# Moving sums, copies and transposes of a transformer block between waits: first sum, delta rule, FFN input, last quarters by token

## The chip, the cores and the metric

The kernel runs on one core of a Trainium2 chip. A core has TensorE (PE, matmuls and transposes), VectorE (DVE), ScalarE (ACT), GpSimd (POOL) and SyncE (SP, which here issues nearly all loads), each with its own instruction queue, and 16 DMA engines that they share. The metric is the device time of one execution in microseconds (us), the median of several.

## The reference, cut to what matters

One layer of a bidirectional encoder, 256 tokens of 2048 channels, all in float32. Two branches run on the same projected input and are merged; a SwiGLU feed-forward part (FFN) follows.

```python
c_act = silu(c)                                   # one row of 2048
mod = c_act @ ada_w + ada_b                       # 6 x 2048: shift, scale, gate of mixer and of FFN
h = rms_norm(x, norm_mix_w) * (1 + scale_m) + shift_m
proj = h @ w_in                                   # q, k, v, gates of both branches
h_a = bidirectional(mlstm_chunkwise, ...)         # branch A: 4 heads, q/k 256, v 512
y_a = (sigmoid(a_o) * rms_norm(h_a)) @ w_branch_a
o_b = bidirectional(gated_delta_chunkwise, ...)   # branch B: 16 heads of 128, gated delta rule
y_b = (rms_norm(o_b) * silu(b_z)) @ w_branch_b
x = x + gate_m * ((g_a * y_a + g_b * y_b) @ w_out)
hf = rms_norm(x, norm_ffn_w) * (1 + scale_f) + shift_f
gt, up = split(hf @ w_gate_up)                    # 2 x 5632
x = x + gate_f * ((silu(gt) * up) @ w_down)
return rms_norm(x, norm_final_w)
```

The delta rule of a chunk needs the inverse of a triangular 64x64 matrix per head, chunk and direction; that is the work called inversion below.

## The kernel before, in words

**Precision.** Every float32 weight matmul is done as three matmuls of a faster 32-bit type: an operand is split into a rounded high part and the rest, and high x high, high x low and low x high are summed. Weights come by 1 MB loads into one ring of three buffers (`raw`); for each half (8 blocks of 128x128, or 2 of 128x512) ScalarE makes the high part (`wh`) and VectorE the low part (`wl`), each in a ring of three. `fjob` (L131, names `b`, `a`) gives outputs with channels on the partitions, two halves to a load; `tjob` (L153, names `z`, `v`, `ma`, `mb`, `o`, `gt`, `up`, `d`) gives outputs with tokens on the partitions: a half is 12 matmuls of 128x512, 6 for each of two token tiles, which end at the same chunk.

**Modulation.** `mod` is not made by TensorE. A row of c is spread over all partitions (`crow`); then for each block of 128 outputs the transposed weights are loaded (1 MB) and VectorE forms one product sum (128x2048, L110 for the parts 2 to 5, L443 and L445 for shift and scale of the mixer). The parts 2 to 5 are a background list: `pump()` is called once for each finished load of weights, and takes one sum of that list at each `every[0]`-th call. The loads of the sums use the `raw` ring and SP's queue as the weights do.

**Stages.** (1) The start, L400 to L455: x is loaded, squared, transposed by TensorE into pxx, copied to x; for each of the 16 channel blocks the two sums, x scaled and shifted, split into hh and hl, and the first 16 projections (`first`). (2) The rest of the projections of branch B in `fill` steps and pieces of a `stream`, between the steps of the delta rule. There are four groups `g` of four heads; each has `gdn_invert` (vector products of small matrices that were reordered through DRAM, inst_d to uu), `gdn_blocks` (copies that lay blocks of 32 rows and columns into R, X and UL) and two pairs `p` of heads in `gdn_phase2`: a chain of small matmuls, copies and products in ten steps, of which the last transposes the normed output (px), scales it (obt, ScalarE) and stores it. `after` and `last` give how many pieces come between two of the steps. (3) mLSTM (branch A), whose head inputs are loaded back from DRAM by SP, between `fill` steps of ma and mb. (4) y_b, y_a, then the output projection o0 to o3 with the residual, each of them one `tjob` for 512 channels. (5) The FFN: x1 is normed (xn), transposed (pxn), scaled and shifted (hf), split into hfh and hfl, two blocks of 128 channels at a time; then gt0, up0, gt1, up1 and so on for 11 groups of 512 channels; then d0 to d3 with the second residual, the final norm and the output.

**What sets the order.** Instructions wrapped in `order(...)` stay as written on their engine's queue; all others are placed by a planner that takes what is ready by its own costs. An engine's queue is strictly in order on the chip: what stands behind a waiting instruction waits with it. `fill(n)` issues n halves of the next projections, `invert(g)` calls it ahead of the inversion.

The line numbers of the profile are those of this kernel. Lines that the prediction's steps touch: L414 to L431 (start), L612 to L616 (UL), L709 to L717 (px and obt), L791 to L796 (invert), L806 (every), L963 to L968 (mLSTM's start), L1021 to L1044 (residual, root, o), L1057 to L1076 (FFN input), L1103 to L1110 (tail).

Of the kernel before, what the change touches and what calls it, by code (L numbers as in the profile page):

```python
# [15 lines left out]
P = 128  # L16
T = 256
# [35 lines left out]
def hybrid_block(ctx: ExitStack, tc: tile.TileContext, xr, nfr, crow, pk_d, cst_d, ada2, ada4, win0, winb, wint, wba, wbb, wo, wgu, wd, out, dbg=None):  # L53
# [44 lines left out]
    for g in range(4):  # L98
        pc_ = acc_ps.tile([P, 512], F32, tag="acc", name=f"crow{g}")
        PE.matmul(pc_, ones[0:1], c1[:, g * 512 : (g + 1) * 512], start=True, stop=True)  # L100
        S.activation(row_c[:, g * 512 : (g + 1) * 512], pc_, AF.Silu)
# [51 lines left out]
    def tjob(name, chunks, xh, xl, done, early=0):  # L153
# [16 lines left out]
        made = [halves(*q) for q in todo[:early]]  # L170
        if early:
            yield True
        ps = [acc_ps.tile([P, 512], F32, tag="acc", name=f"acc_{name}_{t}") for t in range(2)]
        last = 4 * len(chunks) - 1
        for u, k0 in todo:
            wh, wl = made.pop(0) if made else halves(u, k0)
            for k in range(2):
                kk = 4 * u + k0 + k
                for t in range(2):
                    c = slice(t * P, (t + 1) * P)  # L180
                    PE.matmul(ps[t], xh[:, kk, c], wh[:, k], start=kk == 0, stop=False)  # L181
                    PE.matmul(ps[t], xl[:, kk, c], wh[:, k], start=False, stop=False)  # L182
                    PE.matmul(ps[t], xh[:, kk, c], wl[:, k], start=False, stop=kk == last)  # L183
            if k0:
                pump()
                if u == len(chunks) - 1:
                    done(ps)
            yield True

# [215 lines left out]
    with ExitStack() as s0:  # L405
# [9 lines left out]
        junk = w0.tile([P, D + 2], F32, tag="ra", bufs=5, name="junk")  # L415
        for t in range(2):
            order(S.activation(junk[:, :D], xt[t][:, :D], AF.Square, accum_out=ss[:, t : t + 1]))
        order(S.activation(ss, ss, AF.Sqrt, bias=epsc, scale=1.0 / D))
        for b2 in range(KB // 2):
            px = gps(f"pxx{b2}")  # L420
            for e in range(2):
                for t in range(2):
                    PE.transpose(px[:, e * T + t * P : e * T + (t + 1) * P], xt[t][:, (2 * b2 + e) * P : (2 * b2 + e + 1) * P], ident)
            V.tensor_copy(x[:, 2 * b2 : 2 * b2 + 2], px.rearrange("p (e t) -> p e t", e=2))
        V.reciprocal(ss, ss)
        dg = w0.tile([P, T], F32, name="dgx")
        for t in range(2):
            V.tensor_scalar(dg[:, t * P : (t + 1) * P], ident, ss[:, t : t + 1], None, ALU.mult)
        prow = acc_ps.tile([P, 512], F32, tag="acc", name="prow")
        PE.matmul(prow[:, :T], ones, dg, start=True, stop=True)  # L430
# [4 lines left out]
        for b in range(KB):  # L435
            ra = [w0.tile([P, D + 2], F32, tag="ra", bufs=5, name=f"ra{b}_{i}") for i in range(2)]
            raw = st.tile([P, N0, P], F32, tag="raw", bufs=3, name=f"raw0_{b}")
            for i in range(2):
                order(nc.sync.dma_start(ra[i], ada2[b, :, i]))
            order(nc.sync.dma_start(raw, win0[b]))  # L440
            m2 = w0.tile([P, 2], F32, tag="m2", bufs=3, name=f"m2_{b}")
            f = pk[:, PK_NMIX + b : PK_NMIX + b + 1]
            order(V.scalar_tensor_tensor(ra[0], ra[0], f, row_c, ALU.mult, ALU.mult, accum_out=m2[:, 0:1]))  # L443
            order(V.scalar_tensor_tensor(x[:, b], x[:, b], m2[:, 0:1], rows, ALU.mult, ALU.mult))
            order(V.scalar_tensor_tensor(ra[1], ra[1], 1.0, row_c, ALU.mult, ALU.mult, accum_out=m2[:, 1:2]))  # L445
# [145 lines left out]
    def gdn_blocks(g):  # L591
# [20 lines left out]
        for i, a in enumerate((F_, B_)):  # L612
            for b in range(4):
                r = slice(32 * b, 32 * b + 32)
                order(S.activation(UL[r, i, :, r], a[r], AF.Copy))
            yield  # L616

    def gdn_phase2(g, p):
# [91 lines left out]
        for e, on in enumerate(ons):  # L710
            h, hl_ = 4 * g + 2 * p + e, 2 * p + e
            for t in range(2):
                PE.transpose(px[:, (2 * e + t) * P : (2 * e + t + 1) * P], on[:, t], ident)
            obt = bk.tile([P, T], F32, tag="obt", bufs=2, name=f"obt{h}")
# [76 lines left out]
    def invert(g):  # L791
        gen = gdn_invert(g)
        next(gen)
        fill(4)
# [4 lines left out]
    for g in range(4):  # L799
# [6 lines left out]
        every[0] = (0, 2, 2, 2)[g]  # L806
        for p in range(2):
            pieces = stream(4 * g + 2 * p + 4)
# [157 lines left out]
    fill(2)  # L966
    next(cores)
    fill(6)  # L968
# [52 lines left out]
    def residual(t, g, ps, gate, ss, rp):  # L1021
        c = slice(g * 512, (g + 1) * 512)
        tm = rp.tile([P, 512], F32, tag="tm", bufs=2, name=f"tm{ss.name}_{t}_{g}")
        V.tensor_tensor(tm, ps, gate[:, c], ALU.mult)
        V.tensor_tensor(x1[:, t, c], x1[:, t, c], tm, ALU.add)
        S.activation(tm, x1[:, t, c], AF.Square, accum_out=ss[:, t, g : g + 1])

    def token_rstd(ss, name):
        rs = xp.tile([P, 2], F32, name=name)
        V.tensor_reduce(rs, ss, mybir.AxisListType.X, ALU.add)  # L1030
        S.activation(rs, rs, AF.Sqrt, bias=epsc, scale=1.0 / D)
        V.reciprocal(rs, rs)
        return rs

    ss1 = xp.tile([P, 2, 4], F32, name="ss1")
    for g in range(4):
        every[0] = 1 if g in (1, 2) else 2
        run(tjob(f"o{g}", [wo[g, u] for u in range(4)], mgh, mgl, lambda ps: [residual(t, g, ps[t], gm, ss1, wp) for t in range(2)]))
# [4 lines left out]
    every[0] = 4  # L1043
    rs = token_rstd(ss1, "rs1")  # L1044
# [9 lines left out]
    hfl = hp.tile([P, KB, T], F32R, name="hfl")  # L1054
    ffh = fp.tile([P, FB, T], F32R, name="ffh")
    ffl = fp.tile([P, FB, T], F32R, name="ffl")
    for q in range(4):  # L1057
        xn = hp.tile([P, 2, 512], F32, tag="sg", bufs=2, name=f"xn{q}")
        for t in range(2):
            V.tensor_scalar(xn[:, t], x1[:, t, q * 512 : (q + 1) * 512], rs[:, t : t + 1], None, ALU.mult)  # L1060
        for e2 in range(2):
            px = gps(f"pxn{q}_{e2}")
            hf = hp.tile([P, 2, T], F32, tag="hf", bufs=1, name=f"hf{q}_{e2}")
            for e in range(2):
                f = 2 * e2 + e
                for t in range(2):
                    PE.transpose(px[:, e * T + t * P : e * T + (t + 1) * P], xn[:, t, f * P : (f + 1) * P], ident)
                b = 4 * q + f
                V.tensor_scalar(
                    hf[:, e],  # L1070
                    px[:, e * T : (e + 1) * T],
                    affn[:, b : b + 1],
                    mod[:, 3 * KB + b : 3 * KB + b + 1],
                    ALU.mult,
                    ALU.add,
                )  # L1076
            b = 4 * q + 2 * e2
            split(hfh[:, b : b + 2], hfl[:, b : b + 2], hf)

    for j in range(FB // 4):  # L1080
        sg = hp.tile([P, 2, 512], F32, tag="sg", bufs=2, name=f"sg{j}")
        run(tjob(f"gt{j}", [wgu[j, 0, u] for u in range(4)], hfh, hfl,
                 lambda ps: [S.activation(sg[:, t], ps[t], AF.Silu) for t in range(2)]))
# [19 lines left out]
    for g in range(4):  # L1103
        run(tjob(f"d{g}", [wd[g, u] for u in range(KD)], ffh, ffl, lambda ps: [residual(t, g, ps[t], gf, ss2, dp) for t in range(2)]))
    rs = token_rstd(ss2, "rs2")
    for g in range(4):
        c = slice(g * 512, (g + 1) * 512)
        for t in range(2):
            V.scalar_tensor_tensor(x1[:, t, c], x1[:, t, c], rs[:, t : t + 1], nf[:, c], ALU.mult, ALU.mult)
        nc.sync.dma_start(out[:, :, c], x1[:, :, c])  # L1110
# [101 lines left out]
```

## Time and profile before

| | |
|---|---|
| median of 3 runs | 2104.58 us (2102.53 to 2105.44) |
| profiled execution | 2102.55 us, span 2100.8 us |
| mean granted clock of TensorE | 0.986 |
| busy: TensorE, VectorE, ScalarE, GpSimd | 2034.4, 1404.8, 1042.3, 95.8 us |
| loaded from HBM, mean rate | 467 MB, 230 GB/s |

The profile is one execution. Each of its groups names the line, the engine, the operation, the tile written and the tiles read, then how many, busy time and the mean of one in ns, then the engine's idle time just before them and what ended it. "PE px L713 <- ACT obt L715" means that TensorE's instruction of line 713 waited until ScalarE's of line 715 was done. A window row gives for a stretch its length, the busy time of each engine, the clock that was granted to TensorE as a share of full speed, the share of the DMA engines that was busy, and GB/s. Matmuls overlap, so one of them shows a longer time than it adds.

### The profile page before, as it was taken

The page shows a single profiled execution, that of the slowest core. Times are in us where ns is not written, and L with a number is a line of the kernel's source. Part 1 is how long each engine was busy: PE and PEld are TensorE (multiplying, and loading weights), DVE is VectorE, ACT ScalarE, POOL GpSimd, SP SyncE. Part 2 cuts the span into 40 slices and gives each one's busy share as a digit, 9 for nine tenths or more (in the row PEclk, how much of TensorE's full clock was granted, in tenths as well). Part 3 has the DMA queues.
Part 4 walks back from the last instruction along what each step waited for, and adds up shares of the span by engine and source line. Part 5 has one row for each costly group of instructions (what it writes and reads, how often), then busy time and mean ns, then how long its engine had stood idle before and what let it go on. Part 6 is the DMA issues. An engine that isn't in the chain of part 4 may idle for free.

```text
span 2100.8 us, 26981 instructions
## 1 busy us (share of the span) xinstructions
PE 2034.4 (97%) x10374; PEld 1702.8 (81%) x10374; DVE 1404.8 (67%) x2065; ACT 1042.3 (50%) x1546; POOL 95.8 (5%) x189
## 2 busy tenths in 40 slices
PE   8999999999999999999999999899999999999997
PEld 6877789978988888889777877688888888878885
DVE  6787686787877687865677678765556554454544
ACT  2146548756774677565444443344444444444442
POOL 0002210110111011100000000000000000000000
PEclk9999999999999999999999999999999999999999
DMA  9986665566766565767886688566666765555553
GB/s 384 420 315 205 170 210 162 171 189 243 225 195 213 178 213 211 236 247 255 321 298 235 260 288 326 192 220 223 257 223 222 257 206 195 184 198 199 190 190 120
DMA packets 81971, 485.65 MB, mean 231 GB/s; under 512 B 10521, under 2 KB 20001, under 8 KB 27441
## 3 DMA queue, kind: packets, MB, share of 16 engines
q1 hardware_dynamic: 68672, 459.34, 60.9%
q0 software_dynamic: 5856, 9.49, 2.9%
q10 hardware_dynamic: 7314, 15.10, 1.9%
q8 instruction: 81, 1.33, 0.3%
q14 instruction: 48, 0.39, 0.1%
HBM read 467.07 MB, written 16.82 MB: 230 GB/s over the span
## 4 chain that ended last, share of the span: by engine, by line
PE 80%; DVE 7%; DMA 6%; ACT 4%; issue 2%; POOL 0%; SPq 0%; DVEq 0%; ACTq 0%; POOLq 0%
PE acc_gt L181 4%; PE acc_gt L182 4%; PE acc_up L181 4%; PE acc_up L182 4%; PE acc_d L181 4%; PE acc_up L183 4%; PE acc_d L182 4%; PE acc_d L183 4%; PE acc_gt L183 4%; PE first L452 3%; PE acc_b L147 2%; PE acc_b L145 2%; PE acc_b L146 2%; PE acc_o L183 2%; PE acc_o L181 2%; PE acc_o L182 2%
## 5 line engine op out<-in xcount | busy, mean ns | idle before, releaser
L166 DVE TENSOR_TENSOR wl_d<-raw_d,wh_d 128x1024 fp32r<-128x1024 f32 x88 | 107.9, 1226 | 123.2 <-ACT wh_d L165 123.2
L166 DVE TENSOR_TENSOR wl_up<-raw_up,wh_up 128x1024 fp32r<-128x1024 f32 x88 | 107.9, 1226 | 111.7 <-ACT wh_up L165 111.7
L145 PE MATMUL acc_b<-hh,wh_b 128*128 128x256 f32 x576 | 165.2, 287 | 4.7 <-ACT wh_b L141 4.7
L110 DVE SCALAR_TENSOR_TENSOR ada<-ada,crow 128x2048 f32<-128x2048 f32 x64 | 146.4, 2288 | 28.4 <-DMA ada<-ada 28.2
L166 DVE TENSOR_TENSOR wl_gt<-raw_gt,wh_gt 128x1024 fp32r<-128x1024 f32 x88 | 107.2, 1225 | 86.6 <-ACT wh_gt L165 86.6
L147 PE MATMUL acc_b<-hh,wl_b 128*128 128x256 f32 x576 | 162.3, 282 | 1.1 <-DVE wl_b L142 1.1
L165 ACT ACTIVATE wh_d<-raw_d 128x1024 fp32r<-128x1024 f32 x88 | 93.3, 1061 | 138.9 <-PE acc_d L182 134.0
L146 PE MATMUL acc_b<-hl,wh_b 128*128 128x256 f32 x576 | 161.2, 280 | 0.0
L165 ACT ACTIVATE wh_gt<-raw_gt 128x1024 fp32r<-128x1024 f32 x88 | 93.3, 1060 | 133.9 <-PE acc_gt L182 73.4
L165 ACT ACTIVATE wh_up<-raw_up 128x1024 fp32r<-128x1024 f32 x88 | 93.3, 1060 | 117.8 <-PE acc_up L182 82.5
L181 PE MATMUL acc_gt<-wh_gt,hfh 128*128 128x512 f32 x352 | 138.8, 397 | 2.7 <-ACT hfh L205 2.4
L182 PE MATMUL acc_gt<-wh_gt,hfl 128*128 128x512 f32 x352 | 139.4, 396 | 0.0
L183 PE MATMUL acc_gt<-wl_gt,hfh 128*128 128x512 f32 x352 | 138.6, 394 | 0.0
L181 PE MATMUL acc_d<-wh_d,ffh 128*128 128x512 f32 x352 | 137.5, 391 | 0.0
L182 PE MATMUL acc_d<-wh_d,ffl 128*128 128x512 f32 x352 | 137.4, 390 | 0.0
L183 PE MATMUL acc_d<-wl_d,ffh 128*128 128x512 f32 x352 | 137.0, 389 | 0.0
L183 PE MATMUL acc_up<-wl_up,hfh 128*128 128x512 f32 x352 | 136.9, 389 | 0.0
L181 PE MATMUL acc_up<-wh_up,hfh 128*128 128x512 f32 x352 | 136.9, 389 | 0.0
L182 PE MATMUL acc_up<-wh_up,hfl 128*128 128x512 f32 x352 | 136.9, 389 | 0.0
L452 PE MATMUL first<-x,raw 128*128 128x256 f32 x512 | 115.1, 387 | 6.7 <-ACT x L446 6.7
L452 PEld LDWEIGHTS first<-x,raw 128*128 128x128 f32 x512 | 98.7, 194 | 23.0 <-ACT x L446 9.3
L145 PEld LDWEIGHTS acc_b<-hh,wh_b 128*128 128x128 f32 x576 | 110.2, 191 | 5.1 <-ACT wh_b L141 5.1
(345 smaller groups left out, 5256.8 us busy)
## 6 DMA issues: line engine op xcount, KB each, us to landing
ada<-ada SPq DMA_DIRECT2D x64, 1024.0 KB, 5.0
raw_gt<-wgu SPq DMA_DIRECT2D x44, 1024.0 KB, 5.0
raw_up<-wgu SPq DMA_DIRECT2D x44, 1024.0 KB, 4.9
raw_d<-wd SPq DMA_DIRECT2D x44, 1024.0 KB, 4.9
raw_b<-winb SPq DMA_DIRECT2D x36, 1024.0 KB, 5.1
ra<-ada SPq DMA_DIRECT2D x32, 1025.0 KB, 14.6
raw<-win SPq DMA_DIRECT2D x16, 1024.0 KB, 12.8
raw_z<-wint SPq DMA_DIRECT2D x16, 1024.0 KB, 4.9
```

The source lines that it names most:

```text
L110: V.scalar_tensor_tensor(raw, raw, 1.0, row_c[:, :D], ALU.mult, ALU.mult, accum_out=mod[:, c0 + b : c0 + b + 1])
L145: PE.matmul(o, wh[:, k], hh[:, kk], start=kk == 0, stop=False)
L146: PE.matmul(o, wh[:, k], hl[:, kk], start=False, stop=False)
L147: PE.matmul(o, wl[:, k], hh[:, kk], start=False, stop=kk == KB - 1)
L165: order(S.activation(wh, raws[u][:, k0 : k0 + 2], AF.Copy), early)
L166: order(V.tensor_tensor(wl, raws[u][:, k0 : k0 + 2], wh.bitcast(F32), ALU.subtract), early)
L181: PE.matmul(ps[t], xh[:, kk, c], wh[:, k], start=kk == 0, stop=False)
L182: PE.matmul(ps[t], xl[:, kk, c], wh[:, k], start=False, stop=False)
L183: PE.matmul(ps[t], xh[:, kk, c], wl[:, k], start=False, stop=kk == last)
L452: PE.matmul(first[o], raw[:, o], x[:, b], start=b == 0 and o % 2 == 0, stop=b == KB - 1 and o % 2 == 1)
```

## The change

- **Start.** c's row is made in four parts by `c_row`; the square of token tile 0 (ScalarE) stands between the first and the others, that of tile 1 goes to VectorE. `junk`, the squares' unused output, moves from a slot of the `ra` ring into hl, which is written later. The first loads and the sum of scale for block 0 stand ahead of the transposes; the copies of x move from VectorE to ScalarE; the transposes stand behind the scaling of the identity.
- **Delta rule.** Six halves instead of four ahead of the first inversion; the copies of UL's second half (`i == 1`) on VectorE; both heads' transposes ahead of both obt copies; background sums at no piece in the first pair and at each in the second, where they were at every second piece of both (group 0 has none, before and after).
- **mLSTM.** Four halves ahead of the cores' first step, four behind it, instead of two and six.
- **Output projection.** Three sums in each of o0 to o3, at fixed steps. In o3 and d3 the last quarter of the weights (two halves) is done for token tile 0 and then for tile 1 (`by_token`); the residual, the root and, in d3, the final scaling and the output stores of each tile follow its own matmuls. `root()` issues a square root of a constant ahead of o3 and d3. gt0's first two halves are made during o3.
- **FFN input by blocks** of 128 channels with a written order in which each step of gt0 (one half) is issued between the blocks; one in two of the later hf goes to ScalarE. The sums of part 5 begin after gt0.
- **Tail.** nf is multiplied in under the next job for d0 to d2; the output goes in eight parts of 256 KB instead of four of 512 KB.

```diff
+    def c_row(g):
+        order(PE.matmul(pc_, ones[0:1], c1[:, g * 512 : (g + 1) * 512], start=True, stop=True))
+        order(S.activation(row_c[:, g * 512 : (g + 1) * 512], pc_, AF.Silu))
...
-    def tjob(name, chunks, xh, xl, done, early=0):
+    def tjob(name, chunks, xh, xl, done, early=0, by_token=False, steps=1):
...
-        for u, k0 in todo:
+        if by_token:
+            todo = todo[:-2]
+        for n, (u, k0) in enumerate(todo):
             wh, wl = made.pop(0) if made else halves(u, k0)
+            if early and steps > 1 and n + early < len(todo):
+                made.append(halves(*todo[n + early]))
...
+        if by_token:
+            w = [halves(len(chunks) - 1, k0) for k0 in (0, 2)]
+            for t in range(2):
+                for k in range(4):
+                    kk = last - 3 + k
+                    wh, wl = (a[:, k % 2] for a in w[k // 2])
+                    PE.matmul(ps[t], xh[:, kk, c], wh, start=False, stop=False)
...
+                done(t, ps[t])
...
-        junk = w0.tile([P, D + 2], F32, tag="ra", bufs=5, name="junk")
+        junk = hl.rearrange("p b t -> p (b t)")
+        c_row(0)
+        order(S.activation(junk[:, :D], xt[0][:, :D], AF.Square, accum_out=ss[:, 0:1]))
+        for g in (1, 2, 3):
+            c_row(g)
+        order(V.scalar_tensor_tensor(junk[:, D : 2 * D], xt[1][:, :D], 1.0, xt[1][:, :D], ALU.mult, ALU.mult, accum_out=ss[:, 1:2]))
+        order(S.activation(ss, ss, AF.Sqrt, bias=epsc, scale=1.0 / D))
...
+        ra, raw = loads(0)
+        m2 = scale(0, ra)
+        order(V.reciprocal(ss, ss))
...
-            V.tensor_copy(x[:, 2 * b2 : 2 * b2 + 2], px.rearrange("p (e t) -> p e t", e=2))
+            order(S.activation(x[:, 2 * b2 : 2 * b2 + 2], px.rearrange("p (e t) -> p e t", e=2), AF.Copy))
...
-                order(S.activation(UL[r, i, :, r], a[r], AF.Copy))
+                if i:
+                    order(V.tensor_copy(UL[r, i, :, r], a[r]))
+                else:
+                    order(S.activation(UL[r, i, :, r], a[r], AF.Copy))
...
                 PE.transpose(px[:, (2 * e + t) * P : (2 * e + t + 1) * P], on[:, t], ident)
+        for e in range(2):
+            h, hl_ = 4 * g + 2 * p + e, 2 * p + e
             obt = bk.tile([P, T], F32, tag="obt", bufs=2, name=f"obt{h}")
...
-        fill(4)
+        fill(4 if g else 6)
...
-        every[0] = (0, 2, 2, 2)[g]
         for p in range(2):
+            every[0] = p if g else 0
...
-    fill(2)
+    fill(4)
     next(cores)
-    fill(6)
+    fill(4)
...
+        if g == 3:
+            root()
+        for i, _ in enumerate(tjob(f"o{g}", [wo[g, u] for u in range(4)], mgh, mgl, done_o, by_token=g == 3)):
+            if i in ((2, 4, 6) if g < 3 else (1, 2, 4)):
+                sums()
+            if g == 3 and i == 6:
+                next(gt0)
...
+    def moved(b):
+        px = gps(f"pxn{b}")
+        for t in range(2):
+            f = b % 4 * P
+            order(PE.transpose(px[:, t * P : (t + 1) * P], xns[b // 4][:, t, f : f + P], ident))
...
+        if b % 2 and b > 2:
+            order(S.activation(hfs[b], px[:, 0:T], AF.Identity, scale=f, bias=m))
+        else:
+            order(V.tensor_scalar(hfs[b], px[:, 0:T], f, m, ALU.mult, ALU.add))
+        order(S.activation(hfh[:, b], hfs[b], AF.Copy))
+
+    def low(b):
+        order(V.tensor_tensor(hfl[:, b], hfs.pop(b), hfh[:, b].bitcast(F32), ALU.subtract))
...
+    for b in range(2, KB, 2):
+        next(gt0)
+        low(b)
+        if b % 4 == 2 and b < 12:
+            for t in range(2):
+                normed(b // 4 + 1, t, slice(0, 512), S)
+        for e in (b + 2, b + 3):
+            if e < KB:
+                moved(e)
+            if e == b + 2:
+                low(b + 1)
...
+    def finish(t):
+        token_rstd(ss2, rs2, t)
+        r = rs2[:, t : t + 1]
+        for g in (2, 0, 3, 1):
+            o = x1[:, t, g * 512 : (g + 1) * 512]
+            if g == 3:
+                order(V.scalar_tensor_tensor(o, o, r, nf[:, 3 * 512 :], ALU.mult, ALU.mult))
+            elif g == 2:
+                order(V.tensor_scalar(o, o, r, None, ALU.mult))
+            else:
+                order(S.activation(o, o, AF.Copy, scale=r))
+        for g in (2, 0, 3, 1):
+            c = slice(g * 512, (g + 1) * 512)
+            order(nc.sync.dma_start(out[:, t, c], x1[:, t, c]))
```

171 lines of the change are left out of this document (104 added, 67 removed).

## The prediction

> **What bounds the kernel now.** I read the page first (busy shares, then the costliest groups), then TensorE's waits, then windows around the places that the change touches.
>
> ```profile
> span 2100.8 us, 26981 instructions
> PE 2034.4 (97%) x10374; PEld 1702.8 (81%) x10374; DVE 1404.8 (67%) x2065; ACT 1042.3 (50%) x1546; POOL 95.8 (5%) x189
> L166 DVE TENSOR_TENSOR wl_d<-raw_d,wh_d 128x1024 fp32r<-128x1024 f32 x88 | 107.9, 1226 | 123.2 <-ACT wh_d L165 123.2
> L110 DVE SCALAR_TENSOR_TENSOR ada<-ada,crow 128x2048 f32<-128x2048 f32 x64 | 146.4, 2288 | 28.4 <-DMA ada<-ada 28.2
> ```
>
> TensorE (PE) is busy 97% of the span, and the change takes no matmul away. So it can gain only where TensorE stands still or runs at a lower granted clock. Columns below: length of the stretch, busy time of each engine, granted clock, DMA share, GB/s.
>
> ```profile
> core 0: us, PE busy (x) PEld busy (x) DVE busy (x) ACT busy (x) POOL busy (x), PEclk, DMA share, GB/s
> 15.00:20.00 5.00, 2.18 (x12) 1.57 (x10) 4.80 (x8) 1.63 (x3) 0.00 (x0) 0.92 0.71 236
> 20.00:130.00 110.00, 104.83 (x467) 90.35 (x468) 80.86 (x91) 13.86 (x30) 0.00 (x0) 0.96 1.01 421
> 255.00:270.00 15.00, 13.07 (x51) 10.24 (x50) 8.99 (x24) 4.23 (x4) 1.29 (x3) 0.89 0.65 198
> 554.00:604.00 50.00, 50.00 (x405) 47.35 (x404) 43.71 (x83) 35.80 (x73) 5.80 (x12) 1.00 0.66 218
> 610.00:630.00 20.00, 15.73 (x86) 12.88 (x86) 12.12 (x30) 14.52 (x27) 3.46 (x7) 0.91 0.62 178
> 690.00:753.00 63.00, 57.80 (x422) 54.66 (x420) 43.34 (x79) 42.33 (x87) 3.56 (x7) 0.92 0.56 196
> 753.00:817.00 64.00, 62.94 (x456) 57.71 (x456) 55.52 (x111) 44.92 (x91) 5.38 (x10) 1.00 0.66 224
> 996.00:1014.00 18.00, 13.89 (x54) 10.81 (x53) 5.91 (x10) 4.96 (x5) 0.30 (x1) 0.91 0.88 336
> 1284.00:1316.00 32.00, 28.87 (x118) 21.18 (x118) 27.17 (x29) 12.61 (x18) 0.00 (x0) 1.00 0.86 324
> 1335.60:1375.40 39.80, 32.80 (x132) 23.54 (x132) 30.47 (x48) 16.38 (x23) 0.00 (x0) 0.87 0.41 135
> 1400.00:1500.00 100.00, 100.00 (x450) 82.37 (x449) 59.78 (x54) 42.33 (x44) 0.00 (x0) 1.00 0.65 236
> 2085.70:2100.80 15.10, 0.35 (x2) 0.00 (x0) 8.00 (x14) 2.91 (x6) 0.00 (x0) 0.68 0.36 139
> ```
>
> What a stretch loses is its idle time plus its length times what the clock lacks. 996 to 1014: 4.1 idle and 18 x 0.09 = 1.6, so 5.7 us. The costliest stretches are the start of the FFN (7.0 + 5.2), delta-rule group 2 (5.2 + 5.0) and the tail. What TensorE waited for (us, times, longest):
>
> ```profile
> PE acc_b L145 <- ACT wh_b L141: 4.7, 2, 2.6
> PE acc_v L183 <- DVE wl_v L166: 4.7, 3, 1.9
> PE px L713 <- ACT obt L715: 4.2, 2, 3.8
> PE acc_ma L181 <- ACT wh_ma L165: 4.1, 1, 4.1
> PE pa L677 <- ACT UL L615: 1.1, 1, 1.1
> ```
>
> **The change part by part.** Minus is a gain, in us.
>
> *Start.* From 20 to 130 the DMA engines are full (1.01, 421 GB/s); only from 15 to 20 do they fall to 236, because ra loads need the slots of xt (read by the transposes) and junk. With junk moved into hl one load more is issued ahead, and the first sum runs ahead of the transposes. A stage full of DMA ends earlier only by what that hole lost: 5 x (421 - 236)/421 = 2.2. Moving eight copies of x to ScalarE hides under the same transfers (ScalarE 13.86 of 110 busy). Ends: 0 (the hole moves) and -5 (the whole stretch). I take **-2**.
>
> *fill(4) to fill(6) before the first inversion.* From 255 to 270, 1.9 idle and 15 x 0.11 = 1.65 of clock: wl_v is queued on VectorE behind the inversion's first product, which waits for its load. Two more halves of 12 matmuls (100 us hold 450, so 2.7 us each) cover that. Ends 0 and -3.6; **-3**, since 5.4 us of cover exceed the wait.
>
> *Transposes of both heads ahead of the obt copies.* The second head's transposes stood 3.8 us behind the first obt on ScalarE. From 610 to 630: 4.3 idle + 20 x 0.09 = 1.8, so 6.1. Behind the transposes PE next needs wh_z, so up to 1.5 comes back. **-5**, ends -6.1 and -2.
>
> *UL's second four copies to VectorE.* They cost 4 x 0.43 there, in the half of a group that the sums leave:
>
> ```profile
> L615 ACT ACTIVATE UL<-cg 32x256 f32<-32x256 f32 x32 | 13.2, 412 | 0.3
> L666 DVE COPY UL<-p 64x256 f32<-64x256 f32 x8 | 3.4, 428 | 1.6 <-ACT UL L665 1.4
> ```
>
> ScalarE is relieved of 1.65 per group; pa's wait of 1.1 goes. **-1**, ends -1.1 and +1 (VectorE late instead).
>
> *Sums of the delta rule: every second piece in both pairs becomes none in the first pair, one per piece in the second.* In group 2's first pair (690 to 753) PE lost 5.2 + 5.0 = 10.2: on SP's queue an ada load of 1 MB stands ahead of raw_b in a ring of three slots, and on VectorE a sum (2.29 + 0.08) stands ahead of cv. Both go. **-8**, ends -10.2 and -3. In the second pairs it is paid back:
>
> ```profile
> 554.00:604.00 50.00, 7.23 (x7) 1.00 0.66 218
> 753.00:817.00 64.00, 9.20 (x8) 1.00 0.66 224
> ```
>
> Those are the sums alone, for VectorE, in the second pairs of groups 1 and 2. With six there instead (6 x 2.37 = 14.2) VectorE has 43.71 - 7.23 + 14.2 = 50.7 of 50, and 55.52 - 9.20 + 14.2 = 60.5 of 64. It is at its limit in one and near it in the other, and each sum holds a wl and a cv behind it, each of its loads a raw_b. **+4**, ends 0 (buffers even it out) and +16 (each of some seven sums exposed by 2.3).
>
> *mLSTM's start: fill(2), fill(6) to fill(4), fill(4).* The second chunk of raw_ma is issued by SP only here, behind the core's loads (kq, v, o of two heads and ob):
>
> ```profile
> 997.38 2.10 SPq L162 DMA_DIRECT2D raw_ma<-wint  x3
> ```
>
> Hence the wait of 4.1. Two halves ahead of the core cover it. The loads of the core start later by one or two 1 MB transfers and are needed one fill later. 5.7 lost there; **-5**, ends -5.7 and +2.
>
> *Sums in the output projection, 2, 4, 4, 2 per job to 3, 3, 3, 3.* From 1284 to 1316 VectorE has 27.17 of 32, PE idles 3.1. Jobs 1 and 2 lose 2.4 us of VectorE work each. **-2**, ends -3.1 and 0 (job 3 gets a sum more).
>
> *FFN input by blocks, last quarter of o by token, gate 0's first halves early.* Its rows:
>
> ```profile
> 1345.00 1.22 PE L181 MATMUL acc_gt<-wh_gt,hfh 128*128 128x512 f32 x2 [2.39 <-ACT hfh L205]
> L1069 DVE TENSOR_SCALAR hf<-pxn,affn,mod 128x256 f32<-128x256 f32 x16 | 8.7, 542 | 2.0 <-PE pxn L1067 1.7
> L205 ACT ACTIVATE hfh<-hf 128x512 fp32r<-128x512 f32 x8 | 5.1, 632 | 20.1 <-DVE hf L1069 20.1
> L206 DVE TENSOR_TENSOR hfl<-hf,hfh 128x512 fp32r<-128x512 f32 x8 | 5.5, 692 | 4.2 <-ACT hfh L205 4.2
> L447 ACT ACTIVATE hh<-x 128x256 fp32r<-128x256 f32 x16 | 6.7, 416 | 0.5
> L450 DVE TENSOR_TENSOR hl<-x,hh 128x256 fp32r<-128x256 f32 x16 | 6.7, 422 | 0.7 <-ACT hh L447 0.7
> L165 ACT ACTIVATE wh_gt<-raw_gt 128x1024 fp32r<-128x1024 f32 x16 | 16.9, 1057 | 19.5 <-PE acc_gt L182 7.5 <-PE acc_o L182 5.0 <-PE acc_up L182 5.0
> ```
>
> Before, o's last matmul to gate 0's last took 39.8, the first gate matmul 9.4 into it. After, token 1's chain is residual, square, root, xn of 256 columns, transposes and two blocks; wl_gt (1.22) stands in it on VectorE. I make that about 7.0. Then the written order chains every pair of blocks through both engines: hf 0.54, hfh 0.42, hf 0.54, hfh 0.42, wh 1.06, wl 1.22, low 0.42, together 4.6, where PE needs 3.2. Seven such steps and a last one: 7.0 + 32.3 + 3.2 = 42.5, less 0.7 for three more `up` matmuls that lie inside, so **+2**. Ends: -4 (pairs at 3.8, the pace of before) and +11 (about 1.2 more per pair from hand-overs).
>
> *Tail.* Rows of before:
>
> ```profile
> 2085.41 1.37 DVE L1024 TENSOR_TENSOR tmss<-acc_d,gf 128x512 f32<-128x512 f32 x2 [5.39 <-PE acc_d L183]
> 2088.77 1.28 ACT L1031 ACT_TABLE_LOAD   x1
> 2090.06 0.30 ACT L1031 ACTIVATE rs<-rs,epsc 128x2 f32<-128x2 f32 x1
> 2090.59 5.39 DVE L1109 SCALAR_TENSOR_TENSOR x<-x,rs,nf 128x512 f32<-128x512 f32 x8
> 2092.03 4.51 SPq L1110 DMA_DIRECT2D outT<-x  x4
> outT<-x SPq DMA_DIRECT2D x4, 512.0 KB, 3.3
> ```
>
> 15.1 us from the last matmul to the end. After, token 0 ends 2.7 us ahead of the last matmul; token 1 has its residual behind token 0's finish on VectorE (1.4: a scale, a product and two small steps), residual, square and root (2.8: from 2085.41 to 2090.59 is 5.2, less the table load and some 1.1 for the second token), two results on each of two engines (1.2), four issues (1.4, by 4.51 for four that each waited on a product, so at most 1.1 each) and about 3 to land (3.3 for twice the bytes): 9.8. So **-5**, ends -3 and -7. The six nf products done earlier (4.1 us of VectorE) lie in 123 us that it idles before wl_d. [...]
>
> Sum: -2 -3 -5 -1 -8 +4 -5 -2 +2 -5 = **-25**. The profiled execution took 2102.55 (span 2100.8, 1.75 around it); 2077.5. The median of the runs shown is 2.0 higher, which leaves me at **2078**.
>
> **The rivals.**
> *B: the sums saturate VectorE* in the second pairs: +16 instead of +4, so 2090. For it: 50.7 of 50. Against: these pieces have idle ScalarE and three buffers of each half.
> *C: the block chain* costs +11: 2087. For it: strict order on both engines. [...] Against: fewer columns per hand-over start PE sooner.
> *D: the early fills and the start change nothing*, their waits only move: start, first fill, UL and o sums at 0, 2086. For it: DMA full at the start.
> *E: slower.* A sum waits on VectorE for its own load (28.4 us in all before 64 sums), and with one per piece the load is issued right behind a raw_b in a ring of three; wl stands behind. Twelve sums at 2.37 plus a wait of 2.6 each is 60 at most; from 2.9 each (35) upon the other terms' -29 the kernel is slower than before by more than can be told. At 3.2 each: 2112. Against: 554 to 604 shows no PE idle with four.
>
> **How the numbers follow.** Forecast (2066 to 2088) 0.52, B 0.12, C 0.10, D 0.07, all lower ends together (below 2064) 0.04: faster 0.85. About 4 us (0.2%) is what a measurement can tell from no change: same 0.03. E: slower 0.12. The range from 2060 to 2100 leaves out E and a little below.
>
> **What would show it.** The px, acc_ma and pa waits gone from TensorE's list; clock 1.00 from 690 to 753; VectorE near full in second pairs with wl_b or wh_b as a new wait if B or E; gate 0's pairs 4.6 apart if the chain is right, less if not; about 10 us from last matmul to end. The forecast is wrong if the idle time turns up under other names in the same stretches.

## The result and the profile after

The changed kernel takes 2112.35 us (median of 5 runs, 2110.80 to 2115.55) against 2104.58 before (median of 5, 2102.39 to 2105.44). The ratio is 1.0038 with a 95% interval of 1.0020 to 1.0056: slower by some 8 us, where some 27 us faster were forecast. The profiled execution took 2114.81 us (span 2113.0), so its stages add up to 12.2 us over the profile of before, 2.5 more than its median.

The same windows in the changed kernel (columns as in the prediction):

```profile
15.00:20.00 5.00, 2.60 (x15) 2.02 (x14) 3.11 (x5) 2.83 (x7) 0.00 (x0) 1.00 1.02 423
255.00:270.00 15.00, 15.00 (x67) 12.11 (x65) 10.85 (x28) 5.79 (x6) 0.00 (x0) 1.00 0.67 215
610.00:630.00 20.00, 20.00 (x159) 18.52 (x158) 19.78 (x46) 13.45 (x29) 3.54 (x7) 1.00 0.80 249
640.00:656.00 16.00, 11.21 (x38) 8.68 (x38) 8.39 (x23) 3.98 (x5) 0.00 (x0) 0.79 0.49 145
690.00:753.00 63.00, 62.11 (x463) 57.96 (x462) 42.20 (x82) 48.34 (x94) 3.56 (x7) 1.00 0.50 163
753.00:817.00 64.00, 56.39 (x416) 50.91 (x415) 51.83 (x97) 36.85 (x79) 5.38 (x10) 0.97 0.55 197
817.00:832.00 15.00, 9.22 (x32) 6.30 (x31) 13.32 (x31) 12.04 (x17) 0.00 (x0) 0.77 0.86 302
1010.00:1028.00 18.00, 14.26 (x51) 11.34 (x51) 6.71 (x12) 4.63 (x5) 1.06 (x2) 0.81 0.98 376
1349.90:1392.40 42.50, 31.19 (x135) 23.22 (x135) 24.98 (x42) 27.38 (x47) 0.00 (x0) 0.96 0.29 100
2102.10:2113.00 10.90, 0.25 (x2) 0.00 (x0) 4.07 (x9) 3.94 (x8) 0.00 (x0) 0.68 0.51 193
```

Two of these stretches lose time only now; in the kernel before they lost 1.2 us and nothing:

```profile
640.00:656.00 16.00, 14.78 (x86) 12.32 (x85) 15.24 (x33) 8.79 (x10) 1.39 (x3) 1.00 0.58 198
...
817.00:832.00 15.00, 15.00 (x71) 11.68 (x70) 7.67 (x19) 10.41 (x20) 2.17 (x4) 1.00 0.42 144
```

The hole in the DMA share at 15 to 20 is closed, the first inversion's wait is gone, 610 to 630 and 690 to 753 are full at clock 1.00. What the change aimed at in these places, it hit. But 640 to 656, 753 to 817 and 817 to 832 now lose 4.8 + 3.4, 7.6 + 1.9 and 5.8 + 3.5 us (idle, and what the clock lacks). From TensorE's list of waits after:

```profile
PE vps L537 <- ACT vf L284: 7.1, 3, 5.8
PE acc_z L190 <- DVE wl_z L167: 6.7, 4, 4.8
...
PE acc_ma L188 <- ACT wh_ma L166: 4.6, 2, 3.7
...
PE acc_b L147 <- DVE wl_b L142: 4.0, 5, 1.7
PE acc_mb L190 <- DVE wl_mb L167: 3.3, 1, 3.3
```

The waits for px, for pa's UL on ScalarE and most of wh_b have left the list, as forecast; vps, wl_z, wl_b and wl_mb have taken their places. The loss of 640 to 656 is not new time: taken over 604 to 656, TensorE loses about the same in both kernels, 6.6 + 1.6 us before and 4.8 + 3.6 after; it only moved behind the px that the change had cleared. The prediction had named this as a sign of being wrong (idle time under other names in the same stretches). Before, then after:

```profile
604.00:656.00 52.00, 45.45 (x236) 36.93 (x234) 37.04 (x86) 31.76 (x49) 6.07 (x12) 0.97 0.63 190
```

```profile
604.00:656.00 52.00, 47.21 (x286) 40.90 (x285) 40.71 (x93) 29.29 (x57) 7.07 (x14) 0.93 0.68 220
```

VectorE's own waits between 640 and 840 in the changed kernel show what stood ahead of two of these waits:

```profile
DVE utmp L617 <- issue: 7.9, 1, 7.9
DVE wl_b L142 <- ACT wh_b L141: 7.6, 9, 2.6
DVE ada L110 <- DMA ada<-ada: 6.6, 2, 5.4
```

A background sum stood 5.4 us on VectorE for its own load, and wl_mb was queued behind it (3.3 us of TensorE); the inversion's first product stood 7.9 us, with wl_z behind it (4.8). For that one the profile names no releaser ("issue"), so that the sums delayed it is not shown. The wait of vps for ScalarE (5.8, from 818 on) was not followed further.

To see where time came and went by stage, the table takes the same matmul in both traces and subtracts from its time the issue intervals of all matmuls before it, so that a piece of projection done earlier or later does not count. It gives the change in lost time against the profile of before, per stage. A row ends with the matmul that it names: "group 2, first pair" begins in 604 to 656 and ends at the pair's px, which in the changed kernel stands behind the wait for the second pair's first sum (3.3 us and 1.7 of clock). e1 is the first experiment below (the changed kernel with the sums of the delta rule as before).

| stage, up to | forecast | after | e1 |
|---|---|---|---|
| last `first` matmul (start) | -2 | -2.1 | -2.3 |
| group 0's first step (first inversion) | -3 | -3.4 | -3.6 |
| group 0's last px | 0 | +6.7 | +4.6 |
| group 1's last px | -5 (px), -1 (UL) | -1.0 | -0.8 |
| group 2, first pair | -8 | -2.7 | -14.3 |
| group 2, second pair | +4 (with group 1's) | +12.4 | +2.5 |
| group 3's last px | 0 | -1.4 | +3.7 |
| last ma matmul (mLSTM's start) | -5 | +0.8 | +0.9 |
| last y_a matmul | 0 | +2.0 | -0.8 |
| last o matmul (sums in o) | -2 | +3.0 | +4.2 |
| gate 0's last matmul (FFN input) | +2 | +2.1 | +2.3 |
| last d matmul | 0 | -0.1 | 0.0 |
| end (tail) | -5 | -4.1 | -4.1 |
| sum | -25 | +12.2 | -7.7 |

A single profile is no better than some 6 us in the delta rule: e3 below is written as the changed kernel up to mLSTM's start, and had lost 6.2 us less by then (3.2 of them in group 0). The verdicts below rest on timed runs.

### The profile page after: what moved, and what is told of

Read it like the earlier page. It is cut to its first block, busy times and chain, and to the rows that moved or that the text cites. A ratio compares the mean times of both kernels' runs of the same rounds, so it can differ in the third digit from the quotient of the medians.

```text
span 2113.0 us, 27025 instructions
## 1 busy us (share of the span) xinstructions
PE 2037.0 (96%) x10374; PEld 1702.9 (81%) x10374; DVE 1402.2 (66%) x2076; ACT 1051.4 (50%) x1567; POOL 96.0 (5%) x189
## 4 chain that ended last, share of the span: by engine, by line
PE 76%; DVE 9%; DMA 7%; ACT 5%; issue 2%; ACTq 0%; POOL 0%; SPq 0%; DVEq 0%; POOLq 0%
PE acc_up L188 4%; PE acc_up L190 4%; PE acc_up L189 4%; PE acc_d L190 4%; PE acc_d L188 4%; PE acc_d L189 4%; PE acc_gt L190 4%; PE acc_gt L189 4%; PE acc_gt L188 4%; DMA ra<-ada 3%; PE acc_o L190 3%; PE acc_o L188 2%; PE acc_o L189 2%; PE acc_b L145 2%; PE acc_b L147 2%
## 5 line engine op out<-in xcount | busy, mean ns | idle before, releaser
L147 PEld LDWEIGHTS acc_b<-hh,wl_b 128*128 128x128 f32 x576 | 109.4, 190 | 5.6 <-DVE wl_b L142 5.6
```

Of the source, the lines that this page charges most:

```text
L147: PE.matmul(o, wl[:, k], hh[:, kk], start=False, stop=kk == KB - 1)
```

## The experiments

The ratio is always against the kernel before on the same chip, with the 95% interval.

**Which part costs: the changed kernel with one part undone.** e1, the sums of the delta rule:

```diff
+        every[0] = (0, 2, 2, 2)[g]
         for p in range(2):
-            every[0] = p if g else 0
```

> The changed kernel with one part undone: the sums of the delta rule again at every second piece of both pairs (after: none in the first, one per piece in the second). Theory A: these sums, waiting on VectorE for their own loads in the second pairs, are the loss; undone, the second pair of group 2 (TensorE lost 12 us more there) gets it back and its first pair loses its 8 again, with the wait at the next z job gone: 2100 to 2106. Rival B: the two halves more ahead of the first inversion shift which fill meets which wait later; then this run stays within 3 us of the changed kernel (2109 to 2115).

Measured 2097.88 us, 0.9971 (0.9955 to 0.9988), against 1.0038 with the new sums: these cost 14 us. Theory A holds as to the loss (the time is 2 us below its range), and one half of its reasoning does not: the first pair of group 2 should have lost its 8 us again, and it stayed quiet with the sums back in it. In e1's windows:

```profile
690.00:753.00 63.00, 62.34 (x474) 57.99 (x474) 49.42 (x94) 46.43 (x92) 3.49 (x7) 1.00 0.64 223
753.00:817.00 64.00, 59.81 (x430) 54.66 (x428) 54.02 (x115) 46.93 (x99) 5.93 (x11) 0.97 0.58 202
```

e2, the six halves; e3, mLSTM's start; e4, the sums in o:

```diff
-        fill(4 if g else 6)
+        fill(4)
```

> The changed kernel with four halves again ahead of the first inversion. Theory A: worth the 3.4 us won there and no more, so 2114 to 2117. Rival B: the 6.6 us lost in group 0 and the later waits come from that shift, so 2100 to 2107.

Measured 2114.18, 1.0051 (1.0034 to 1.0068): no gain from undoing it, so the shift is not what made the kernel slower. Its trace shows one thing more. It has four halves as the kernel before, but no sums in the first pair, and there the waits for wh_b are gone too: of the 4.2 us that are still idle, 3.1 are the wait for the second pair's first sum.

```profile
690.00:753.00 63.00, 58.83 (x446) 55.00 (x445) 41.44 (x80) 46.91 (x93) 3.57 (x7) 1.00 0.47 151
```

```diff
-    fill(4)
+    fill(2)
     next(cores)
-    fill(4)
+    fill(6)
```

> The changed kernel with two halves ahead of mLSTM's first step and six behind, as before. The prediction's step (worth 5 us) gives 2115 to 2119; my reading now, that the same raw_ma load still stands behind the core's loads and the wait has only moved, gives 2110 to 2114 and a wait of about 4 us either way.

Measured 2114.95, 1.0044 (1.0021 to 1.0067): worth nothing within 4 us. The wait is the same in both, 3.7 us; of e3, around mLSTM's start:

```profile
PE acc_ma L188 <- ACT wh_ma L166: 3.7, 1, 3.7
```

```diff
+        every[0] = 1 if g in (1, 2) else 2
...
-            if i in ((2, 4, 6) if g < 3 else (1, 2, 4)):
-                sums()
```

> The changed kernel with the sums of the output projection again by the count of pieces (2, 4, 4, 2 per job instead of 3, 3, 3, 3). The prediction's step (worth 2 us) gives 2113 to 2116; the trace (o lost 2.9 us more after the change) gives 2108 to 2111.

Measured 2111.34, 1.0032 (1.0014 to 1.0049), as the changed kernel: neither the forecast's gain nor the loss that I read from the trace. What o's first job loses (1.7 to 6.4 us by the same matmul in the changed kernel and all forms of it, 2.6 in e4) is not these sums; e15 to e18 below, forms of the kernel before, lose 0 to 1.7 there. What it is was not followed up.

**With the sums out of the way: e1 with one more part undone.** e5 puts back the FFN boundary as it was before: o3 not by token, no early halves of gate 0, pairs of blocks placed by the planner.

```diff
-        for i, _ in enumerate(tjob(f"o{g}", [wo[g, u] for u in range(4)], mgh, mgl, done_o, by_token=g == 3)):
+        for i, _ in enumerate(tjob(f"o{g}", [wo[g, u] for u in range(4)], mgh, mgl, done_o)):
...
-            if g == 3 and i == 6:
-                next(gt0)
...
-    for t in range(2):
-        normed(0, t, slice(0, 256), V)
...
+    for q in range(4):
+        xn = hp.tile([P, 2, 512], F32, tag="sg", bufs=2, name=f"xn{q}")
...
+            split(hfh[:, b : b + 2], hfl[:, b : b + 2], hf)
```

> e1 (sums of the delta rule as before) with the FFN boundary undone too: o3 not by token, gate 0's halves not made early, the FFN input in pairs of blocks placed by the planner. Equal work, counted in e1's profile, took 2.3 us more from o's last matmul to gate 0's last than before, so 2 us less than e1: 2094 to 2097. If the written block order is free or a gain: 2098 to 2102.

Measured 2093.80, 0.9949 (0.9927 to 0.9972): 4 us less than e1 by the medians, in the direction of the forecast's +2, with intervals that overlap.

e6 puts back only the FFN input in pairs; o3 by token and the early halves stay:

```diff
-    for t in range(2):
-        normed(0, t, slice(0, 256), V)
...
+    for q in range(4):
...
+            split(hfh[:, b : b + 2], hfl[:, b : b + 2], hf)
```

> e1 with only the block order undone: o3 by token and gate 0's early halves stay, the FFN input is done in pairs of blocks placed by the planner. If the written chain of about 4.6 us per pair is the loss and the early start (2 us) a gain, this is 3 to 5 us below e1 and 2 below e5: 2093 to 2095. If the chain isn't it: as e1, 2097 to 2099.

Measured 2115.28, 1.0040 (1.0024 to 1.0056): 17 us more than e1. Both expectations fail. In it the early halves of gate 0, in written order, stand between the planner's copies, and TensorE loses 17 idle and 15 of clock in this stretch:

```profile
1330.00:1400.00 70.00, 52.91 (x210) 40.87 (x211) 40.61 (x52) 24.96 (x31) 0.00 (x0) 0.78 0.41 147
```

So the early halves of gate 0 need the written block order; it is a slow chain, but half of the edit is much worse. e7 and e8 undo the px order and the UL copies:

```diff
                 PE.transpose(px[:, (2 * e + t) * P : (2 * e + t + 1) * P], on[:, t], ident)
-        for e in range(2):
-            h, hl_ = 4 * g + 2 * p + e, 2 * p + e
```

> e1 with each head's transposes again directly ahead of its obt copy. The prediction's step (5 us) gives 2102 to 2104, with the wait of px for obt back at about 4 us. The rival, that this wait was only the place where some 4 us were lost and not its cause, gives 2097 to 2100.

Measured 2093.23, 0.9944 (0.9926 to 0.9963): not slower than e1. The wait of px for obt comes back, but at 1.4 us, where it was 4.2 in the kernel before. Of e7:

```profile
PE px L757 <- ACT obt L759: 1.4, 2, 1.2
```

```diff
-                if i:
-                    order(V.tensor_copy(UL[r, i, :, r], a[r]))
-                else:
-                    order(S.activation(UL[r, i, :, r], a[r], AF.Copy))
+                order(S.activation(UL[r, i, :, r], a[r], AF.Copy))
```

> e1 with all copies of UL on ScalarE again. The prediction's step (1 us) gives 2098 to 2100. If the freed ScalarE is what removed the 10 us of waits in group 2's first pair (its sums are not: e1 has them and no waits there), 2105 to 2109 and that stretch shows a clock below 1 again.

Measured 2093.79, 0.9951 (0.9935 to 0.9968): no loss either. Both steps that the prediction priced at a gain are worth nothing, or cost up to 4 us, once the rest stands. e9 undoes the six halves on top of e1:

```diff
-        fill(4 if g else 6)
+        fill(4)
```

> e1 (sums of the delta rule as before) with four halves instead of six ahead of the first inversion. e1, e7 and e8 all lack the 10 us of waits in group 2's first pair, with or without the changed px order and UL copies; what they share in that stage is the six halves. If the shift by two halves is what removed those waits: 2106 to 2113, waits and a clock below 1 back between 690 and 753. If the six halves are worth only the 3 us at the first inversion: 2100 to 2102.

Measured 2104.73, 0.9998 (0.9980 to 1.0016): 6 us more than e1, and the waits of group 2's first pair are back. Of e9:

```profile
690.00:753.00 63.00, 57.52 (x419) 54.03 (x419) 45.53 (x87) 42.60 (x85) 3.48 (x7) 0.95 0.59 204
```

So two halves done 430 us earlier remove the ten microseconds lost there before, with the sums in place (e1); taking the sums out removes them as well, without the two halves (e2). Either is enough, and with both the gain is had once. e10 undoes the sums, the FFN boundary, px and UL together (the edits of e1, e5, e7 and e8):

> e1 with three more parts undone, those that cost by the runs so far: FFN boundary (4), px order (4), UL copies (4). If they add up: 2086 to 2090. If px and UL share one cause: 2089 to 2093. If they only differed by noise: 2094 to 2098.

Measured 2091.45, 0.9934 (0.9911 to 0.9957): faster than both kernels, and the costs do not add up (e5, e7 and e8 would promise 12 us below e1; it is 6).

**What in a sum costs.** Two forms of the changed kernel, all parts in it:

```diff
-            V.scalar_tensor_tensor(raw, raw, 1.0, row_c[:, :D], ...)
+            V.scalar_tensor_tensor(raw[:, 0:128], raw[:, 0:128], 1.0, row_c[:, 0:128], ...)
```

> The changed kernel (all parts) with the sum of every background block over 128 of its 2048 columns, so VectorE spends 0.3 us in place of 2.3 on each of 64; the 1 MB loads and their waits stay; the rest of each sum is left out. If VectorE's time for the sums is what costs 14 us: 2092 to 2098 or less. If it is the wait for their loads and the slots of the raw ring: 2106 to 2112.

```diff
-            nc.sync.dma_start(raw, ada4[part - 2, b])
-            V.scalar_tensor_tensor(raw, raw, 1.0, row_c[:, :D], ...)
+            nc.sync.dma_start(raw[:, 0:128], ada4[part - 2, b][:, 0:128])
+            V.scalar_tensor_tensor(raw, row_c[:, :D], 1.0, row_c[:, :D], ...)
```

> The changed kernel with only 128 of the 2048 columns loaded for each background sum (64 KB in place of 1 MB), while VectorE forms a product sum of full length from c's row with itself, so the sums are not those wanted; buffers and order stay. If the wait for the load and SP's queue cost the 14 us: 2092 to 2100. If VectorE's time does: 2108 to 2113.

Measured 2091.84, 0.9934 (0.9910 to 0.9958), and 2095.64, 0.9948 (0.9932 to 0.9965). Each alone gives 17 to 20 us by the medians, more than undoing the sums' new places. Both shorten the sums of the later stages too, and short sums in their old places were not run, so how much of these 17 to 20 us belongs to the delta rule is not known from the times. The traces say more. Group 2's second pair with what precedes and follows it, in the changed kernel, e1, e11 and e12, in that order:

```profile
745.00:832.00 87.00, 73.61 (x486) 63.92 (x485) 69.11 (x138) 56.19 (x110) 6.73 (x13) 0.94 0.62 213
```

```profile
745.00:832.00 87.00, 82.48 (x539) 73.13 (x538) 69.29 (x147) 57.11 (x110) 8.07 (x15) 0.98 0.61 212
```

```profile
745.00:832.00 87.00, 81.56 (x525) 70.84 (x524) 62.20 (x152) 58.19 (x112) 8.07 (x15) 0.96 0.66 237
```

```profile
745.00:832.00 87.00, 79.96 (x515) 69.77 (x516) 73.05 (x151) 58.72 (x113) 8.07 (x15) 0.96 0.46 154
```

Idle and clock together, they lose 18.6, 6.3, 8.9 and 10.5 us. With a sum at each piece, either short form takes back most of what the dense sums cost here, though not all. The first sum of the pair shows how. In the changed kernel it waits 5.4 us for its load and then takes 2.3, and TensorE waits 3.3 for the wl_mb behind it. With the operation short VectorE waits as long (5.5) and TensorE 1.2; with the load short VectorE waits 3.2 and TensorE 1.0. So neither rival is right by itself: in this wait the long load and the long operation stand one behind the other. e13 turns the sums round:

```diff
-            every[0] = p if g else 0
+            every[0] = 1 - p if g else 0
```

> The changed kernel with its sums turned round: at each piece of the first pair, none in the second. Shorter operations alone or shorter loads alone both took the loss away, so it needs load and VectorE together. If any pair with a sum per piece is too full: 2108 to 2116. If it is the place (the end of the second pair, with the next group's inversion and z job behind): 2094 to 2103.

Measured 2113.24, 1.0057 (1.0038 to 1.0076), as slow as the changed kernel. The loss moves to the first pair (e13's window; 8.7 idle, 5.0 of clock):

```profile
690.00:753.00 63.00, 54.28 (x401) 51.26 (x400) 46.38 (x81) 35.42 (x74) 2.99 (x7) 0.92 0.54 196
```

It is the density of a sum per piece, not the pair that it is put in, that costs.

**Single parts.** e14 is e10 with mLSTM's start undone:

```diff
-    fill(4)
+    fill(2)
     next(cores)
-    fill(4)
+    fill(6)
```

> e10 (sums, FFN boundary, px order and UL copies as before) with mLSTM's start undone too. If that step is worth nothing: as e10, 2088 to 2094. If it is worth the 5 us of the prediction: 2094 to 2099.

Measured 2089.81, 0.9941 (0.9921 to 0.9961): as e10; that step is worth nothing in a quiet kernel either. The wait is still 4.3 us there. e15 is the kernel before with one line changed:

```diff
-        fill(4)
+        fill(4 if g else 6)
```

> The kernel before with one part added: six halves ahead of the first inversion. If the shift by two halves alone removes the waits of group 2's first pair: 2094 to 2100, with about 60 busy of 63 and clock 1.00 from 690 to 753. If it is worth only the wait at the first inversion: 2100 to 2103.

Measured 2095.15, 0.9959 (0.9943 to 0.9976): one line gives some 9 us (7 by the medians). e16 is the kernel before with nothing but the new sums:

```diff
-        every[0] = (0, 2, 2, 2)[g]
         for p in range(2):
+            every[0] = p if g else 0
```

> The kernel before with one part added: sums of the delta rule at no piece of the first pair and each of the second. If they cost the 14 us by themselves: 2114 to 2122. If only together with the shift by two halves: 2100 to 2108. The prediction's step (worth 4): 2099 to 2102.

Measured 2116.65, 1.0069 (1.0047 to 1.0091): 14.5 us slower, by themselves. Group 2's first and second pair in e16:

```profile
690.00:753.00 63.00, 58.66 (x443) 54.69 (x442) 42.52 (x83) 46.72 (x94) 3.58 (x7) 0.98 0.48 162
753.00:817.00 64.00, 56.82 (x415) 51.08 (x414) 54.45 (x104) 40.17 (x83) 5.39 (x10) 0.95 0.62 225
```

The first pair loses 5.6 us where the kernel before lost 10.2, and 3.3 of the 5.6 are TensorE's wait behind the second pair's first sum; the second pair loses 10.4, where it lost 1.1.

e17 and e18 are e15 with eight and with five halves:

```diff
-        fill(4)
+        fill(4 if g else 8)
```

> The kernel before with eight halves ahead of the first inversion. If six gained 9 us because the first inversion is covered and the work that follows has more in hand, eight gain the same: 2092 to 2097. If the gain is that of which piece of projection meets which wait (a phase), eight is another phase and may lie anywhere between 2092 and 2108; outside 2092 to 2097 decides for it.

```diff
-        fill(4)
+        fill(4 if g else 5)
```

> The kernel before with five halves ahead of the first inversion. If cover counts: half of six's gain, 2096 to 2101. If the phase counts: outside of that, and the waits of group 2's first pair either fully there (4 to 5 us for wh_b) or gone.

Eight: 2103.47, 0.9991 (0.9973 to 1.0009). Five: 2095.64, 0.9960 (0.9941 to 0.9979). Group 2's first pair with six, eight and five halves, in that order:

```profile
690.00:753.00 63.00, 60.90 (x446) 56.15 (x445) 49.15 (x98) 47.76 (x98) 3.58 (x7) 0.97 0.59 201
```

```profile
690.00:753.00 63.00, 57.73 (x422) 53.61 (x421) 45.02 (x75) 41.33 (x85) 2.21 (x4) 0.97 0.54 193
```

```profile
690.00:753.00 63.00, 61.44 (x458) 56.91 (x457) 50.41 (x91) 49.25 (x97) 3.57 (x7) 1.00 0.64 226
```

Four and eight have the waits there (5.2 and 5.3 idle), five and six hardly (1.6 and 2.1). Eight cover the first inversion as well as six do (its window from 255 to 270 is full), so cover is not what counts. What is left is the phase: which piece of the projections comes to which step of the delta rule. Why this piece and not that one makes a wait there was not settled.

## Why the prediction was wrong

It was wrong in sign. The step that failed is **"Sums of the delta rule": -8 in the first pair and +4 in the second.** By itself it is +14.5 (e16), undone in the changed kernel it is 14 (e1). The +4 was far too low, and the -8 was not to be had beside the six halves.
- The gain of 8 was read from a wait's neighbours: an ada load ahead of raw_b on SP, a sum ahead of cv on VectorE. By itself that reading holds: with four halves, the waits for wh_b leave the first pair when the sums do (e2, e16). But e1 and e15 keep the sums in that pair and lack the waits, with six halves; e9 has the waits back with four halves and the sums. In the changed kernel the six halves had taken this gain already, which the prediction had priced only at their own place (-3), and the sums were moved for nothing.
- The cost of 4 came from filling up VectorE's busy time (50.7 of 50). That was a good sign of danger and a bad price. VectorE is not busier over 753 to 817 than before (51.83 against 55.52): it waits. The first sum of the pair held what is behind it on VectorE for its own load as well as for its operation (5.4 and 2.3 us: wl_mb, whose wh_mb was done at 751.1, began at 756.9), and e11 and e12 show that with one of the two short most of the loss is gone. The upper end that I kept (+16) is near the truth; rival B had put its price there. Rival E named the mechanism, a sum that waits for its load with wl behind it, and asked for 2.9 us per sum; at the twelve sums that it counted, the 14.5 us are 1.2 each. The kernel came out slower only since the other terms were much smaller than forecast, and that E's 2112 for 3.2 per sum is the measured time is luck.

**The terms that were not there.** px (-5), UL (-1), mLSTM (-5) and the sums in o (-2) are worth about nothing: e7, e8, e3 and e14, e4. For px and UL the wait was real and left the list, but it goes as well when only the phase changes: e15, the kernel before with six halves, has no wait of px for obt, and e7, with the old px order and six halves, has 1.4 of the 4.2 us. Over 604 to 656, around that px, e15 has the old order and six halves and loses 1.6 us; e9 has the new order and four halves and loses 9.4, where the kernel before lost 8.1. For mLSTM the mechanism failed: the second chunk of raw_ma is still issued behind the core's loads, two halves later, and the wait came along (1010 to 1028: 3.7 idle, clock 0.81). Of the 13 us of these four, none appeared.

**The first inversion** (-3): right in its place, -3.4 by the same matmul, and under-sized as a step of the whole: alone it gives 9 us (e15), for a reason I had not seen, the waits of group 2's first pair. What it gains in its own place is given back in group 0: every kernel with six halves loses 3.4 to 6.7 us more there than the kernel before, e15 (+3.6) included, while those with four and eight lose the same as before (within 0.6).

**The start** (-2): right in sign, with the DMA share at 1.02 where it was 0.71; that it measures -2.1 is in part luck. e15 to e18 have the start of the kernel before, and at the same matmul they too stand 0.8 to 2.1 us below its profile; all kernels with the new start stand 2.1 to 2.5 below. So about 1 us is the change's, and the rest is one slow start in the profile of before.

**The FFN input** (+2): right in mechanism; the size is open. The stretch from o's last matmul to gate 0's last takes 42.5 us, as worked out. The chain that ended last, from 1361 on, repeats at 4.7 us per pair, where I worked out 4.6:

```profile
1361.43 1.23 DVE wl_gt L167
1363.10 0.55 DVE hf L1162
1363.68 0.43 ACT hfh L1163
1364.10 0.56 ACT hf L1160
1365.11 0.96 ACT wh_gt L166
1366.09 1.23 DVE wl_gt L167
...
1370.04 0.95 ACT wh_gt L166
1371.02 1.23 DVE wl_gt L167
```

By the same matmul it is +2.1; by e5 about 4 with the rest of the boundary, within overlapping intervals. But e5, e10 and e14, which have the boundary undone, still show +1.3 to +2.0 in this stage, so of the +2.1 about 1 us or less is shown to be the chain's. The pairs lost no clock: it is 1.00 from 1361.0 to 1392.4, where TensorE's longest wait is 1.2 us.

**The tail** (-5): right, -4.1; 11.0 us from the last matmul to the end in place of 15.1, where I had 9.8. Token 1's chain is as long as I took it, and eight issues on SP took 6.0:

```profile
2102.07 0.29 ACT L1081 ACTIVATE rs<-rs,epsc 128x1 f32<-128x1 f32 x1 [0.23 <-DVE rs L1080]
2103.11 6.03 SPq L1232 DMA_DIRECT2D outT<-x  x8
2106.57 1.33 ACT L1229 ACTIVATE x<-x,rs 128x512 f32<-128x512 f32 x2 [0.23 <-DVE rs L1082]
```

No table load stands before the root now.

One step of the sum does not follow: 25 us below the median of 2104.58 is 2079.6, not 2078. It changes nothing here.

The chances were wrong too: 0.12 for slower was given to one mechanism, while four terms rested on the same unproved reading, that a wait which is named in the list goes away for good when what it names is moved.

## What to carry to other kernels

A wait in the list is a place and not yet a cause: when background pieces fill the gaps of a dependent chain, a shift of the pieces can move the waits, and here one line was worth 9 us, or nothing, depending on a phase that no busy time shows (four, five, six, eight halves: 1, 0.996, 0.996, 0.999). Price a sum or a copy by its operation and by its own load's wait together (2.3 and 5.4 us for the first sum of group 2's second pair), and keep it sparse: at every second piece the second pair of group 2 lost 1.1 us over 753 to 817, at each piece 10.4 (e16), and 14.5 in the whole kernel. Two edits that remove the same wait gain it once: ask of each what it gives with the other in place. Try the parts of such a change one by one: the six halves alone beat the whole change by some 17 us. Of the kernels that leave no work out, e10 (0.9934; it keeps the start, the six halves, mLSTM's start, the sums in o and the tail) and e14 (0.9941) are the fastest, though their intervals overlap that of the six halves alone (0.9959).

## What the runs showed of the hardware that was not expected

Two executions in which TensorE's instructions stand in the same order (the changed kernel and e3, up to mLSTM) differ by 6.2 us of lost time, 3.2 of it in one stage, and ten runs of e1 span 2090.73 to 2106.64; a stage's loss read from one profile is uncertain by several us.

Around each of the seven waits of 1.9 to 5.8 us named below, the granted clock is half for a while, as here at the end of the wait of 4.8 us in the changed kernel:

```profile
650.00:652.00 2.00, 1.96 (x5) 1.58 (x6) 1.83 (x7) 0.00 (x0) 0.00 (x0) 0.50 0.00 0
```

The price does not follow the length of the wait. In the changed kernel, waits of 4.8, 5.8 and 3.7 us cost 3.4 us of clock each: 640 to 656, clock 0.79; 817 to 832, 0.77; 1010 to 1028, 0.81. In windows of 1 us the clock reads 0.78, 0.50 six times and 0.81 from 648 to 656, so about 6.8 us at half clock, and as much in the other two. In the kernel before, waits of 3.8 and 4.1 us cost half of that (610 to 630 and 996 to 1014, clock 0.91 in both: 1.8 and 1.6), and so did one of 1.9 us (255 to 270, 0.89: 1.7; from 264 to 269 the windows of 1 us read 0.97, 0.50 three times and 0.82, so about 3.4 us at half clock). What sets these lengths is not shown. The first wait at the FFN's input, 4.4 us, left the clock at 0.85 over 1349.9 to 1361.0, and that is the whole of the 0.96 over 1349.9 to 1392.4: in the pairs from 1361.0 on, with waits of at most 1.2 us, it is 1.00.
